# Scores of two mLSTM heads in turn, from the two row halves of the array, and exponents of two heads made ahead

## The chip, the core and the metric

The kernel runs on one core of a Trainium2 chip. Its engines are PE (TensorE: matmuls; PEld is its weight load), DVE (VectorE), ACT (ScalarE), POOL (GpSimd) and SP, which issues loads. The metric is the device time of one launch in microseconds (us). A difference of 0.2% is about what the measurement can tell from none.

## What is computed

A decoder layer on 512 positions of width 1024: an mLSTM branch and a sparse-attention branch, merged by gates, then a gated feed-forward network. The change lies in the mLSTM branch, which has four heads (q and k 64 wide, v 128 wide). The reference works in chunks of 64; what it comes to for one head is

```python
b = jnp.cumsum(logf, axis=-1)
D = b[..., :, None] - b[..., None, :] + i_pre[..., None, :]
D = jnp.where(causal, D, NEG)
m_t = jnp.maximum(inter, jnp.max(D, axis=-1))
Dw = jnp.exp(D - m_t[..., None])
s = jnp.einsum('bhctd,bhcsd->bhcts', q, k) * Dw
num = isc[..., None] * jnp.einsum('bhctd,bhcde->bhcte', q, C_prev) + jnp.einsum('bhcts,bhcse->bhcte', s, v)
h = num / jnp.maximum(jnp.abs(den), jnp.exp(-m_t))[..., None]
```

after which each head is normalised over its 128 columns and multiplied by `sigmoid(mo)`.

## The kernel before, in words

The kernel works on the whole 512x512 lower triangle of a head at once, in tiles of 128x128: four tiles of keys j, and for each the queries i >= j. Products of float32 numbers are made of three matmuls, on a rounded part (h) and a remainder (l): kh·qh, kh·ql, kl·qh.

PE is fed in an order that is written out by hand. Between the steps of a chain the code calls `fill(ns)`, which issues matmuls of an independent stream, in triples of 128x512, until their nominal length (650 for a triple) has used up `ns`. While the heads run, the stream is the projection `gn`: eight tiles gn0 to gn7 of 24 matmuls (lines 489 to 491), two PSUM buffers of the pool `pa` in turn. A finished tile is copied out by ACT (line 709), some triples later in ACT's program order. Its weights are split three tiles ahead by ACT (lines 88 and 91) and a DMA that adds (line 92). Behind the `gn` stream comes the stream `un` (lines 509 to 511). The lengths stand in the table `PLAN`. Each engine executes its own instructions in program order.

One head h goes through these steps (names as in the code and the rows):

- `mls_s`: PE makes the row-max term `mb` with one matmul of 36 rows (line 1087) and the scores with twelve matmuls of 64 rows (lines 1095 to 1097), into two PSUM tiles `mA` and `mB` of the pool `s` (two buffers of two banks). q and k of heads 0 and 2 lie in rows 0 to 63 of a tile `mq`, those of heads 1 and 3 in rows 64 to 127.
- `mls_e` (line 1106): DVE adds `mb` and a column, and takes the minimum with 0, in ten pieces of 128x128, into the SBUF tiles EA and EB. `mls_x`: ACT takes exp of both (lines 1112 and 1113), POOL masks the diagonal tiles (line 1116).
- `mls_m` (lines 1121 and 1122): DVE multiplies scores and exponentials.
- `mls_b`: PE makes the outputs `mo` (line 1129: ten products, each of which runs as two matmuls of 128x129) in the PSUM tiles of the pools `pt` and `po`, which have one buffer each. ACT takes the absolute value of the denominator (1134), DVE a maximum and a reciprocal (1135, 1137), ACT four squares (1142), DVE and ACT the inverse root (`rstd`, lines 382 to 388), and DVE scales into `hs` (1150). In the middle of it, `mid` starts `mls_s`, `mls_e` and `mls_x` of the next head.
- `mls_c`: PE transposes `hs` in four matmuls into `mhT` (line 1158), in the one buffer of `pt`; DVE multiplies it with a gate (1159), ACT and DVE split the product (1160, 1161).

Head 0's scores, exponents and products stand ahead of the loop over heads. Behind head 3's `mls_b` the `gn` stream is run to its end, if it has any left, and `un` takes over.

Of the kernel before, what the change touches and what calls it, by code (L numbers as in the profile page):

```python
# [10 lines left out]
ALU = mybir.AluOpType  # L11
# [4 lines left out]
P = 128  # L16
S = 512
D = 1024
NT = S // P
# [78 lines left out]
def bcast(ap, n):  # L98
# [30 lines left out]
def FL(key, default):  # L129
    return PLAN.get(key, default)  # L130


PD = dict(A=0, C=2, MV=2, GM=2, MO=2, MQK=2, GN=0, UN=0, UM=0, WO=0)

# [26 lines left out]
def body(ctx, tc, I, out, dbg=None):  # L161
    nc = tc.nc
    act, dve, pe, pool = nc.scalar, nc.vector, nc.tensor, nc.gpsimd
# [39 lines left out]
    def lpage(name, dt=F32):  # L203
        return ar.tile([P, 2064], dt, name=name, tag="pm", bufs=1)

    def s4(name, dt=F32):
        return ar.tile([P, 1024], dt, name=name, tag="s4", bufs=6)
# [4 lines left out]
    def psS(name):  # L212
        return ps.tile([P, 1024], F32, name=name, tag="s", bufs=2)
# [13 lines left out]
    T = {}  # L227
# [63 lines left out]
    W.on_pool = {T_B[c] for c in range(4) if FL(f"q2_pb{c}", (1, 0, 0, 0)[c])}  # L291
    for nm, ids in (("A", T_A), ("C", T_C), ("MV", T_MV), ("GM", F_GM), ("MO", F_MO), ("MQK", F_MQK), ("GN", F_GN),
                    ("UN", F_UN), ("UM", F_UM), ("WO", T_WO[:4])):
# [71 lines left out]
    for tl, names in ((vrow, (("merge_gate_b", 16), ("m_conv_w", 16), ("m_conv_b", 4), ("m_out_norm_w", 4))),  # L365
                      (vrow2, (("ffn_conv_w", 3 * NF), ("ffn_conv_b", NF)))):
        r = 0
        for nm, n in names:
            a = I[nm]
# [84 lines left out]
    def tok_accs(name):  # L454
        a0, a1, s = pa(name + "0"), pa(name + "1"), psS(name + "s")
        return [a0[:, :], a1[:, :], s[:, 0:512], s[:, 512:1024]]

    def tok_group(ids, n, accs, evac, flag):
        cost = 650 * n / 512
        W.ensure(ids[0])  # L460
        for c, i in enumerate(ids):
            H, L = W.hl[i]
            order = [(t, kk) for t in range(NT) for kk in range(2)]
            if 0 < c < 3:
                order.sort(key=lambda e: e[1])
            for z, (t, kk) in enumerate(order):
                k = 2 * c + kk
                if z == FL("q8_ens" + flag, 4):
                    W.ensure(i + 3)
                mm3(accs[t][:, :n], act4(hTH, k, t * P, (t + 1) * P), act4(hTL, k, t * P, (t + 1) * P),  # L470
                    H[:, kk, :], L[:, kk, :], k == 0, k == KD - 1)
                if k == KD - 1:
                    d = FL("q4_aft" + flag, 1) + 1
                    after(d, lambda t=t: evac(t, accs[t]))
                    if t == NT - 1:
                        after(d, lambda: done.add(flag))
                yield cost
                tick()
# [255 lines left out]
    def proj_stream():  # L734
        yield from tok_group(T_C, 288, tok_accs("aC"), evac_c, "C")
        yield from tok_group(T_A, 512, tok_accs("aA"), evac_a, "A")
        T["mv1"] = lpage("mv1").rearrange("p (t h c) -> p t h c", t=NT, h=4)
# [10 lines left out]
    fill = Filler(proj_stream(), flush)  # L748
# [329 lines left out]
        dve.tensor_copy(uoc, p[:, 0:40])  # L1078
        act.activation(emc, p[:, 40:56], AF.Exp, scale=-1.0)

    def mls_s(h):
        r0 = slice((h % 2) * 64, (h % 2) * 64 + 64)
        mq = T["mq"][h // 2][r0]
        A = psS(f"mA{h}")
        B = psS(f"mB{h}")
        mb = B[:, 0:512]
        pe.matmul(mb, sel[:, h, :], T["nHL"], start=True, stop=True)
        at = [A[:, 0:512], A[:, 512:896], B[:, 768:1024], B[:, 512:768]]
        for j in range(NT):
            ks = slice(j * P, (j + 1) * P)  # L1090
            kh, kl = mq[:, 1, ks], mq[:, 3, ks]

            q0 = min(j, NT - 2) * P
            qh, ql = mq[:, 0, q0:], mq[:, 2, q0:]
            pe.matmul(at[j], kh, qh, start=True, stop=False)
            pe.matmul(at[j], kh, ql, start=False, stop=False)
            pe.matmul(at[j], kl, qh, start=False, stop=True)
        return A[:, 0:896], B[:, 640:1024], mb

    def mls_e(h, sc):  # L1100
        mb = sc[2]
        EA, EB = s4(f"EA{h}"), s4(f"EB{h}")
        et = [EA[:, 0:512], EA[:, 512:896], EB[:, 128:384], EB[:, 0:128]]
        for k, (i, j) in enumerate(pairs):
            e = et[j][:, (i - j) * P:(i - j + 1) * P]
            dve.tensor_scalar(e, mb[:, i * P:(i + 1) * P], uoc[:, k * 4 + h:k * 4 + h + 1], 0.0,
                              op0=ALU.add, op1=ALU.min)
        return EA[:, 0:896], EB[:, 0:384], et

    def mls_x(ee):  # L1110
        EA, EB, et = ee
        act.activation(EA, EA, AF.Exp)
        act.activation(EB, EB, AF.Exp)
        for j in range(NT):
            e = et[j][:, 0:P]
            pool.affine_select(e, e, pattern=[[1, P]], compare_op=ALU.is_ge, fill=0.0, base=0,
                               channel_multiplier=-1)

    def mls_m(sc, ee):
        EA, EB, et = ee  # L1120
        dve.scalar_tensor_tensor(EA, sc[0], 0.125, EA, op0=ALU.mult, op1=ALU.mult)
        dve.scalar_tensor_tensor(EB, sc[1], 0.125, EB, op0=ALU.mult, op1=ALU.mult)

    def mls_b(h, et, mid):
        o = [pt(f"mo{h}0"), po(f"mo{h}1")]
        ov = [o[i // 2][:, (i % 2) * 129:(i % 2) * 129 + 129] for i in range(NT)]
        for i in range(NT):
            for j in range(i + 1):
                pe.matmul(ov[i], et[j][:, (i - j) * P:(i - j + 1) * P], T["mv1"][:, j, h, :],
                          start=(j == 0), stop=(j == i))  # L1130
        nxt = mid[0]()
        ad = sm([P, 4], "mad")
        for z in range(2):
            act.activation(ad[:, 2 * z:2 * z + 2], o[z][:, :258].rearrange("p (b c) -> p b c", b=2)[:, :, P], AF.Abs)
        dve.tensor_max(ad, ad, emc.rearrange("p (t h) -> p t h", h=4)[:, :, h])
        rec = sm([P, 4], "mrec")
        dve.reciprocal(rec, ad)
        hp = s4(f"hs{h}")
        hs, junk = hp[:, 0:512], hp[:, 512:640]
        ss = sm([P, 4], "mss")  # L1140
        for i in range(NT):
            act.activation(junk, ov[i][:, 0:P], AF.Square, scale=rec[:, i:i + 1],
                           accum_out=ss[:, i:i + 1])
        ne = mid[1](nxt)
        rs = sm([P, 4], "mrs")
        rstd(rs, ss, 4, 1.0 / P)
        mid[2](ne)
        dve.tensor_mul(rs, rs, rec)
        for i in range(NT):
            dve.tensor_scalar(hs[:, i * P:(i + 1) * P], ov[i][:, 0:P], rs[:, i:i + 1], None, op0=ALU.mult)  # L1150
        return hs, nxt, ne
# [36 lines left out]
    fill(FL("z19", 1950))  # L1188
    fill.until(done, "A")

# [50 lines left out]
        fill(FL("z25", 1300))  # L1241
    act.preload_act_table_set(LNEXP)
    T["hmH"] = v4(page("hmH", F32R))
    sc = mls_s(0)
    ee = mls_e(0, sc)
    mls_x(ee)
    fill(FL("ms0", 5000))
    mls_m(sc, ee)
    for h in range(4):
        if h < 3:  # L1250
            mid = (lambda: mls_s(h + 1), lambda n: mls_e(h + 1, n), mls_x)
        else:
            mid = (lambda: None, lambda n: None, lambda n: None)
        fill(FL(f"mb{h}", 1000))
        hs, sc, ee = mls_b(h, ee[2], mid)
        if h == 3:
            fill.until(done, "GN")
            fill = Filler(up_group(F_UN, T["onH"], T["onL"], evac_un, "un", "UN", (1, 3, 6, 7)), flush)
            W.ensure(F_UN[3])
            act.preload_act_table_set("sigmoid_and_others")  # L1260
            for i in range(2):
                for z in range(2):
                    g = T["gn"][i][:, 2 * z:2 * z + 2, :]
                    act.activation(g, g, AF.Sigmoid)
        fill(FL(f"mc{h}", 5000))
        if h == 2:
            mls_m(sc, ee)
        mls_c(h, hs)
        if h == 3:
            for i in range(2):  # L1270
                for z in range(2):
                    fill(1300)
                    g = T["gm"][i][:, 2 * z:2 * z + 2, :]
                    act.activation(g, g, AF.Sigmoid)
            act.preload_act_table_set(LNEXP)
        if h < 2:
            fill(FL(f"md{h}", 2000))
            mls_m(sc, ee)
    fill.until(done, "UN")


# [22 lines left out]
    fill = Filler(up_group(F_UM, T["hmH"], T["hmL"], evac_um, "um", "UM", (1, 6, 7)), flush)  # L1304
# [339 lines left out]
```

## Time and profile before

| | us |
|---|---|
| timed runs | 782.43, 783.40, 783.75 (median 783.4) |
| the profiled execution | 782.3 |
| its span, from the first to the last instruction | 780.6 |
| PE busy | 773.1 (99%) |
| DVE busy | 468.4 (60%) |
| ACT busy | 373.9 (48%) |
| POOL busy | 208.1 (27%) |

The profile is one execution. Busy time is the union of an engine's records. Matmuls are pipelined: a record begins where the matmul is issued and ends, by a model, where its last column has left, so that records overlap and the distance of two starts tells how long one holds the engine. Waits are named by the line that released them. The heads run from 285 to 352 us of the span.

### The profile page before, as it was taken

To read this page: it belongs to the slowest core of one execution; us is meant where nothing else is said; L and a number is where in the kernel's file an instruction comes from. 1 tells how busy PE (TensorE), PEld (TensorE's weight loads), DVE (VectorE), ACT (ScalarE), POOL (GpSimd) and SP (SyncE) were. 2 spreads that over 40 slices of the span, in tenths; PEclk is the share of its full clock that TensorE was granted. 3 is DMA by queue.
4 is the path that set the end of the run, shared out by engine and by line. 5 is a ranking of instruction groups with operands and counts; after the bars stand their busy time and mean duration, and the time that the engine had idled before them with its cause. 6 is when DMAs were issued, how large, how long until landed. Compare 5 with 4: busy or idle time off the path is not lost.

```text
span 780.6 us, 10546 instructions
## 1 busy us (share of the span) xinstructions
PE 773.1 (99%) x4037; PEld 641.0 (82%) x4037; DVE 468.4 (60%) x826; ACT 373.9 (48%) x630; POOL 208.1 (27%) x220
## 2 busy tenths in 40 slices
PE   8999999999999999999999999999999999999998
PEld 6797888778888888888888988888888888888886
DVE  5476785676566664566627365555545454566865
ACT  6254546645565685475624253333443433455441
POOL 3320131220111122110200037745555542200700
PEclk9999999999999999999999999999999999999999
DMA  6984069665656476543687168664455533675472
GB/s 232 295 224 140 7 127 170 109 110 107 109 100 117 87 104 135 107 136 108 145 290 249 45 217 307 226 246 171 182 216 193 183 122 150 213 276 185 148 237 87
DMA packets 93892, 129.03 MB, mean 165 GB/s; under 512 B 6512, under 2 KB 72208, under 8 KB 92433
## 3 DMA queue, kind: packets, MB, share of 16 engines
q1 hardware_dynamic: 63054, 91.64, 35.0%
q0 software_dynamic: 30784, 36.70, 22.8%
q8 instruction: 32, 0.52, 0.3%
q14 instruction: 20, 0.16, 0.1%
q10 hardware_dynamic: 2, 0.00, 0.0%
HBM read 94.79 MB, written 15.73 MB: 142 GB/s over the span
## 4 chain that ended last, share of the span: by engine, by line
PE 93%; DVE 4%; issue 1%; ACT 1%; POOL 0%; DVEq 0%; POOLq 0%
PE ff L1361 10%; PE ff L1360 10%; PE ff L1359 10%; PE P L428 4%; PE P L429 4%; PE P L427 4%; PE on L937 2%; PE ptp L926 2%; PE gn L489 2%; PE gn L491 2%; PE gn L490 2%; PE wo L429 2%; PE wo L428 2%; PE wo L427 2%; PE gm L489 1%; PE gm L491 1%
## 5 line engine op out<-in xcount | busy, mean ns | idle before, releaser
L94 DVE TENSOR_TENSOR whl<-raw,whl 128x1024 fp32r<-128x1024 f32 (+2 forms) x109 | 137.7, 1275 | 149.8 <-ACT whl L88 149.7
L88 ACT ACTIVATE whl<-raw 128x1024 fp32r<-128x1024 f32 (+2 forms) x144 | 144.8, 1012 | 126.4 <-PE ff L1361 57.3
L1359 PE MATMUL ff<-h2H,whl 128*128 128x512 f32 (+1 forms) x384 | 142.8, 372 | 0.0
L1360 PE MATMUL ff<-h2L,whl 128*128 128x512 f32 (+1 forms) x384 | 142.6, 371 | 0.0
L1361 PE MATMUL ff<-h2H,whl 128*128 128x512 f32 (+1 forms) x384 | 142.6, 371 | 0.0
L92 POOL DMA_DIRECT2D whl<-raw x34 | 47.0, 1384 | 231.8 <-ACT whl L91 181.5
L1360 PEld LDWEIGHTS ff<-h2L,whl 128*128 128x128 f32 x384 | 72.3, 188 | 12.6
L1359 PEld LDWEIGHTS ff<-h2H,whl 128*128 128x128 f32 x384 | 72.3, 188 | 12.5
L1361 PEld LDWEIGHTS ff<-h2H,whl 128*128 128x128 f32 x384 | 72.3, 188 | 12.4
L911 ACT ACTIVATE P<-sp,nmx 128x128 f32<-128x128 f32 (+3 forms) x64 | 33.1, 523 | 36.8 <-DVE nmx L902 36.5
L1411 ACT ACTIVATE ct<-ct 128x512 f32<-128x512 f32 x22 | 13.9, 633 | 54.1 <-DVE ct L1409 54.1
L902 DVE TENSOR_REDUCE nmx<-sp 128x2 f32<-128x256 f32 (+3 forms) x32 | 26.2, 818 | 17.9 <-PE sp L899 17.8
L91 ACT ACTIVATE whl<-raw 128x1024 fp32r<-128x1024 f32 x34 | 35.7, 1050 | 0.0
L427 PE MATMUL P<-whl,g 128*128 128x512 f32 x88 | 34.2, 389 | 0.0
L428 PE MATMUL P<-whl,g 128*128 128x512 f32 x88 | 34.2, 389 | 0.0
L429 PE MATMUL P<-whl,g 128*128 128x512 f32 x88 | 34.2, 389 | 0.0
L1409 DVE SCALAR_TENSOR_TENSOR ct<-ff,vcol,ct 128x511 f32<-128x511 f32 (+1 forms) x44 | 32.7, 744 | 2.2 <-ACT ct L1407 1.4
L1417 ACT ACTIVATE g<-ct 128x512 fp32r<-128x512 f32 x22 | 13.9, 632 | 36.9 <-DVE ct L1421 21.9
L235 DVE COPY P<-ptp 128x256 f32<-128x256 f32 (+1 forms) x32 | 17.7, 554 | 18.6 <-PE ptp L926 18.5
L1418 DVE TENSOR_TENSOR g<-ct,g 128x512 fp32r<-128x512 f32 x22 | 15.4, 699 | 21.9 <-ACT g L1417 21.9
L489 PE MATMUL gm<-hTH,whl 128*128 128x512 f32 x64 | 26.6, 416 | 0.0
L428 PE MATMUL P<-whl,sb 128*128 128x512 f32 x66 | 25.9, 393 | 0.2
(399 smaller groups left out, 1781.0 us busy)
## 6 DMA issues: line engine op xcount, KB each, us to landing
raw<-in_ffn_w_up_dram SPq DMA_DIRECT2D x22, 1024.0 KB, 5.0
whl<-raw POOLq DMA_DIRECT2D x34, 512.0 KB, 5.7
raw<-in_w_in_dram SPq DMA_DIRECT2D x16, 1024.0 KB, 5.0
st<-in_ffn_w_down_dram SPq DMA_DIRECT2D x11, 1024.0 KB, 7.1
td<-st POOLq DMA_DIRECT2D x11, 1024.0 KB, 4.1
raw<-td SPq DMA_DIRECT2D x22, 512.0 KB, 5.3
raw<-in_ffn_w_down_dram SPq DMA_DIRECT2D x11, 512.0 KB, 4.1
raw<-in_w_out_dram SPq DMA_DIRECT2D x4, 1024.0 KB, 4.7
```

The lines of the kernel that those rows point to most:

```text
L88: nc.scalar.activation(h, src, AF.Copy)
L91: nc.scalar.activation(l, src, AF.Copy, scale=-1.0)
L92: nc.gpsimd.dma_start(l, src, accum_op=ALU.add)
L94: (nc.gpsimd if n in self.on_pool else nc.vector).tensor_sub(l, src, h)
L427: pe.matmul(o, aH, bH, start=start, stop=False)
L428: pe.matmul(o, aH, bL, start=False, stop=False)
L429: pe.matmul(o, aL, bH, start=False, stop=stop)
L489: pe.matmul(acc, H[:, k, :], hh, start=(k == 0), stop=False)
L911: act.activation(Pv[:, y], sv[:, y], AF.Exp, bias=nmx[:, y:y + 1], accum_out=den[:, y:y + 1])
L1359: pe.matmul(acc[:, a:b], H[:, k, :], hh, start=(k == 0), stop=False)
L1360: pe.matmul(acc[:, a:b], H[:, k, :], hl, start=False, stop=False)
L1361: pe.matmul(acc[:, a:b], L[:, k, :], hh, start=False, stop=(k == KD - 1))
```

## The change

The scores of heads 0 and 1, and of heads 2 and 3, are issued in turn, one matmul of the lower and one of the upper row half. `mls_sA` makes the tiles j = 0 and 1 of two heads (each head in a PSUM tile of its own) and multiplies them; `mls_sB` does the same for j = 2 and 3 (one PSUM tile, a bank for each head). The row-max matmul gets a PSUM tile of its own (`mls_mb`), and DVE's exponent pieces read it there. Ahead of the loop, row-max terms and exponents of heads 0 and 1 are made, then their scores. Inside `mls_b` of heads 0 and 1 the row-max term and the exponents of heads 2 and 3 follow; their scores stand behind `mls_c(1)`. Fillers are spread anew.

```diff
-    "mc0": 4675, "mc1": 5000, "mc2": 5000, "mc3": 11500, "md0": 3950, "md1": 3625, "md2": 0, "ms0": 6300,
+    "mc0": 5850, "mc1": 5850, "mc2": 5850, "mc3": 11500, "md0": 3900, "md1": 1950, "md2": 34800, "ms0": 6500,
...
-    def mls_s(h):
...
+    def mls_mb(h):
+
+        mb = psS(f"mM{h}")[:, 0:512]
         pe.matmul(mb, sel[:, h, :], T["nHL"], start=True, stop=True)
...
+    def mls_s(p, js, at):
+
+        mq = T["mq"][p]
+        for j in js:
+            ks = slice(j * P, (j + 1) * P)
+
+            q0 = min(j, NT - 2) * P
+            for n, (kk, qq) in enumerate(((1, 0), (1, 2), (3, 0))):
+                for z in range(2):
+                    r = slice(z * 64, z * 64 + 64)
+                    pe.matmul(at[z][j], mq[r, kk, ks], mq[r, qq, q0:], start=(n == 0), stop=(n == 2))
+
+    def mls_sA(p, ees):
+        A = [psS(f"mA{2 * p + z}") for z in range(2)]
+        mls_s(p, (0, 1), [(a[:, 0:512], a[:, 512:896]) for a in A])
+        for z in range(2):
+            dve.scalar_tensor_tensor(ees[z][0], A[z][:, 0:896], 0.125, ees[z][0], op0=ALU.mult, op1=ALU.mult)
+
+    def mls_sB(p, ees):
+        B = psS(f"mB{p}")
+        b = [B[:, z * 512:z * 512 + 512] for z in range(2)]
+        mls_s(p, (2, 3), [{2: a[:, 256:512], 3: a[:, 0:256]} for a in b])
+        for z in range(2):
+            dve.scalar_tensor_tensor(ees[z][1], b[z][:, 128:512], 0.125, ees[z][1], op0=ALU.mult, op1=ALU.mult)
...
-    sc = mls_s(0)
-    ee = mls_e(0, sc)
-    mls_x(ee)
-    fill(FL("ms0", 5000))
-    mls_m(sc, ee)
+    none = (lambda: None, lambda n: None, lambda n: None)
+    mbs = [mls_mb(z) for z in range(2)]
+    ees = {z: mls_e(z, mbs[z]) for z in range(2)}
+    for z in range(2):
+        mls_x(ees[z])
+    fill(FL("ms0", 6500))
+    mls_sA(0, (ees[0], ees[1]))
+    fill(FL("ms1", 1950))
+    mls_sB(0, (ees[0], ees[1]))
+    fill(FL("ms2", 1300))
     for h in range(4):
-        if h < 3:
-            mid = (lambda: mls_s(h + 1), lambda n: mls_e(h + 1, n), mls_x)
-        else:
-            mid = (lambda: None, lambda n: None, lambda n: None)
-        fill(FL(f"mb{h}", 1000))
-        hs, sc, ee = mls_b(h, ee[2], mid)
+        mid = none
+        if h < 2:
+            mid = (lambda: mls_mb(h + 2), lambda n: mls_e(h + 2, n), mls_x)
+        hs, _, ne = mls_b(h, ees[h][2], mid)
+        if h < 2:
+            ees[h + 2] = ne
...
-        if h == 2:
-            mls_m(sc, ee)
         mls_c(h, hs)
...
-        if h < 2:
+        if h == 1:
+            mls_sA(1, (ees[2], ees[3]))
+            fill(FL("ms3", 2600))
+            mls_sB(1, (ees[2], ees[3]))
+        if h < 3:
             fill(FL(f"md{h}", 2000))
-            mls_m(sc, ee)
```

On PE at the start of the heads, before: behind the row-max matmul and the scores of head 0 come 30 fillers (the rest of gn1, gn2, three of gn3), then head 0's outputs.

```order
L1087 MATMUL mB0_2879<-mrowC_1771,sel_176 128x512 [waits Pool_49]
L1095 MATMUL mA0_2878<-mq0_2813 128x512 [waits Activation_49]
L1096 MATMUL mA0_2878<-mq0_2813 128x512 [waits DVE_49]
...
L1097 MATMUL mB0_2879<-mq0_2813 128x256
L489 MATMUL gn1_2835<-hTH1_140,whl33_2634 128x512
...
L489 MATMUL gn3_2944<-hTH0_139,whl35_2817 128x512 [waits Activation_49]
...
L1129 MATMUL mo00_2950<-mv1_944,EA0_2893 128x129 [waits DVE_49,PE_49]
```

The same place now: two row-max matmuls, 30 fillers, and the scores of heads 0 and 1 in turn.

```order
L1084 MATMUL mM0_2878<-mrowC_1771,sel_176 128x512 [waits Pool_49]
L1084 MATMUL mM1_2880<-mrowC_1771,sel_176 128x512
L489 MATMUL gn1_2835<-hTH1_140,whl33_2634 128x512
...
L489 MATMUL gn3_2951<-hTH0_139,whl35_2817 128x512 [waits Activation_49]
L490 MATMUL gn3_2951<-hTL0_141,whl35_2817 128x512
L491 MATMUL gn3_2951<-hTH0_139,whl35_2817 128x512 [waits DMASW7_49]
L1106 MATMUL mA0_2955<-mq0_2813 128x512 [waits DVE_49,PE_49]
L1106 MATMUL mA1_2956<-mq0_2813 128x512 [waits DVE_49,PE_49]
```

The scores moved from ahead of the fillers to behind them; gn3, which waits for ACT, stands 27 fillers behind the row-max matmuls, as it stood 27 behind the scores.

On ACT at the same place, before: the exponentials of head 0, then the copy of filler tile gn1.

```order
L1242 ACT_TABLE_LOAD
L1112 ACTIVATE EA0_2893<-EA0_2893 128x896 [waits DVE_49]
L1113 ACTIVATE EB0_2894<-EB0_2894 128x384 [waits DVE_49,Activation_49]
L709 ACTIVATE gn0_2794<-gn1_2835,vcol_132 128x512 [waits PE_49]
L88 ACTIVATE whl37_2928<-raw18_2734 128x1024 [waits DMASW5_49]
```

And now:

```order
L1248 ACT_TABLE_LOAD
L1123 ACTIVATE EA0_2882<-EA0_2882 128x896 [waits DVE_49]
L1124 ACTIVATE EB0_2883<-EB0_2883 128x384 [waits DVE_49,Activation_49]
L1123 ACTIVATE EA1_2894<-EA1_2894 128x896 [waits DVE_49,Activation_49]
L1124 ACTIVATE EB1_2895<-EB1_2895 128x384 [waits DVE_49]
L709 ACTIVATE gn0_2794<-gn1_2835,vcol_132 128x512 [waits PE_49]
L88 ACTIVATE whl37_2935<-raw18_2734 128x1024 [waits DMASW5_49]
```

The copy of gn1 moved behind the exponentials of two heads.

On PE at the end of the heads, before: between head 2's outputs (`mo2`) and its transposes (`mhT2`) stand head 3's row-max matmul and scores and 24 fillers; between the transposes and head 3's outputs (`mo3`) stand 12.

```order
L1129 MATMUL mo21_3222<-mv1_944,EB2_3126 128x129 [waits Pool_49]
L1087 MATMUL mB3_3234<-mrowC_1771,sel_176 128x512
L1095 MATMUL mA3_3233<-mq1_2814 128x512
...
L489 MATMUL gn6_3205<-hTH1_140,whl38_3035 128x512
...
L491 MATMUL gn7_3310<-hTH0_139,whl39_3074 128x512
L1158 MATMUL mhT2_3326<-ident_96,hs2_3254 128x128 [waits DVE_49,Activation_49]
...
L489 MATMUL gn7_3310<-hTH1_140,whl39_3074 128x512
...
L1129 MATMUL mo30_3352<-mv1_944,EA3_3260 128x129 [waits DVE_49,Pool_49]
```

The same place now: 9 fillers, the last of gn7, in the first gap, none in the second, and behind head 3's outputs the stream un.

```order
L1135 MATMUL mo21_3297<-mv1_944,EB2_3035 128x129 [waits Pool_49]
L489 MATMUL gn7_3259<-hTH1_140,whl39_3088 128x512
...
L491 MATMUL gn7_3259<-hTH1_140,whl39_3088 128x512
L1164 MATMUL mhT2_3346<-ident_96,hs2_3314 128x128 [waits DVE_49,Activation_49]
L1164 MATMUL mhT2_3346<-ident_96,hs2_3314 128x128
L1164 MATMUL mhT2_3346<-ident_96,hs2_3314 128x128 [waits DVE_49] x2
L1135 MATMUL mo30_3354<-mv1_944,EA3_3162 128x129 [waits DVE_49,Pool_49]
...
L1135 MATMUL mo31_3355<-mv1_944,EB3_3163 128x129 [waits Pool_49]
L509 MATMUL un0_3402<-onH_1543,whl40_3129 128x512
```

The scores of head 3 and 27 fillers moved out of this stretch to places ahead of it.

## Rows read from the trace of the kernel before

**Rows 1.** The page, the chain that ended last, by engine.

```profile
PE 93%; DVE 4%; issue 1%; ACT 1%; POOL 0%; DVEq 0%; POOLq 0%
```

**Rows 2.** Windows: stretch, length, busy us of PE, PEld, DVE, ACT, POOL, PEclk, DMA.

```profile
285.00:339.40 54.40, 54.34 (x295) 45.78 (x293) 30.53 (x93) 33.34 (x71) 13.01 (x22) 1.00 0.63 118
```

**Rows 3.** Timeline of PE, head 0: start, length, line, tiles, shape.

```profile
284.50 0.39 PE L491 MATMUL gn<-hTH,whl 128*128 128x512 f32 x1
...
285.18 0.39 PE L491 MATMUL gn<-hTH,whl 128*128 128x512 f32 x1
285.50 0.50 PE L1087 MATMUL mB<-mrowC,sel 36*128 36x512 f32 x1
285.83 0.40 PE L1095 MATMUL mA<-mq 64*128 64x512 f32 x1
...
287.07 0.28 PE L1095 MATMUL mB<-mq 64*128 64x256 f32 x1
...
288.20 0.39 PE L490 MATMUL gn<-hTL,whl 128*128 128x512 f32 x1
```

**Rows 4.** Timeline of PE, head 1.

```profile
296.60 0.61 PE L1129 MATMUL mo<-mv,EB 128*128 128x129 f32 x4
297.14 0.49 PE L1087 MATMUL mB<-mrowC,sel 36*128 36x512 f32 x1
297.14 0.49 PE L1095 MATMUL mA<-mq 64*128 64x512 f32 x1
297.48 0.39 PE L1096 MATMUL mA<-mq 64*128 64x512 f32 x1
...
299.62 0.39 PE L490 MATMUL gn<-hTL,whl 128*128 128x512 f32 x1
```

**Rows 5.** Timeline of DVE, head 0.

```profile
285.45 1.29 DVE L1236 TENSOR_TENSOR mq<-cv,mq 128x512 fp32r<-128x512 f32 x2 [1.08 <-ACT mq L1233]
287.98 1.90 DVE L1106 TENSOR_SCALAR EA<-mB,uoc 128x128 f32<-128x128 f32 x7 [1.23 <-PE mB L1097]
289.79 0.86 DVE L1106 TENSOR_SCALAR EB<-mB,uoc 128x128 f32<-128x128 f32 x3
```

**Rows 6.** Timeline of ACT, head 0.

```profile
290.77 0.51 ACT L1113 ACTIVATE EB<-EB 128x384 f32<-128x384 f32 x1
291.19 0.67 ACT L709 ACTIVATE gn<-gn,vcol 128x512 f32<-128x512 f32 x1
```

**Rows 7.** Timeline of all engines, head 3's outputs and `hs`.

```profile
339.01 0.61 PE L1129 MATMUL mo<-mv,EB 128*128 128x129 f32 x4
...
339.69 0.40 PE L510 MATMUL un<-onL,whl 128*128 128x512 f32 x1
...
344.05 1.13 DVE L1150 TENSOR_SCALAR hs<-mo,mrs 128x128 f32<-128x128 f32 x4
```

**Rows 8.** Timeline of all engines, head 0's `hs` and transposes.

```profile
303.64 1.13 DVE L1150 TENSOR_SCALAR hs<-mo,mrs 128x128 f32<-128x128 f32 x4
...
303.95 0.39 PE L491 MATMUL gn<-hTH,whl 128*128 128x512 f32 x1
...
304.40 0.76 PE L1158 MATMUL mhT<-ident,hs 128*128 128x128 f32 x4
...
304.91 0.48 PE L489 MATMUL gn<-hTH,whl 128*128 128x512 f32 x1
...
305.19 0.75 DVE L1159 SCALAR_TENSOR_TENSOR hs<-mhT,vcol,mo 128x512 f32<-128x512 f32 x1 [0.42 <-PE mhT L1158]
```

**Rows 9.** Timeline of PE, the start, to the longest idle of PE.

```profile
10.69 0.63 PE L428 MATMUL aB<-whl,hTH 128*128 128x512 f32 x1
11.11 0.44 PE L429 MATMUL aB<-whl,hTL 128*128 128x512 f32 x1
11.39 0.39 PE L427 MATMUL aB<-whl,hTH 128*128 128x512 f32 x1
...
14.01 0.31 PE L420 MATMUL pn<-ident,x 128*128 128x128 f32 x1 [0.38 <-issue]
```

More of the change, by code (lines that the diff above doesn't have):

```diff
@@ L1079, in rows_b, with mls_e @@
         act.activation(emc, p[:, 40:56], AF.Exp, scale=-1.0)
-    def mls_s(h):
[L1082 to L1086, printed above, removed]
-        pe.matmul(mb, sel[:, h, :], T["nHL"], start=True, stop=True)
[L1088 to L1101, printed above, removed]
+    def mls_mb(h):
+        mb = psS(f"mM{h}")[:, 0:512]
+        pe.matmul(mb, sel[:, h, :], T["nHL"], start=True, stop=True)
+        return mb
+    def mls_e(h, mb):
         EA, EB = s4(f"EA{h}"), s4(f"EB{h}")
@@ L1117, in mls_x @@
                                channel_multiplier=-1)
[L1119 to L1122, printed above, removed]
     def mls_b(h, et, mid):
```

## Prediction

> **What bounds the kernel now.** I read the page first: its chain that ended last is 93% PE [rows 1]. A busy PE need not be a well-used one, so next I asked for the stretch of the four mLSTM heads by windows: PE busy 54.34 of 54.40 us, PEclk 1.00, DVE and ACT busy for 30.53 and 33.34 us [rows 2]. So PE sets the end here. What an edit saves on PE comes off the end, what makes PE wait goes onto it, and work on DVE or ACT counts only where PE waits for it. Matmul records overlap (their ends are modelled), so from here on I read PE by its starts: a 128x512 filler matmul starts every 0.227 us, (285.18-284.50)/3 [rows 3].
>
> The PE timeline of head 0 prices one block of scores [rows 3]. From the last filler at 285.18 to the second filler behind the block at 288.20 are 3.02 us; less two filler steps that is 2.57. Inside: 0.227 for the row-max matmul (36 rows); 1.24 for the six matmuls of 512 and 384 columns (285.83 to 287.07), called A; and, since 285.18 to 285.83 is two normal steps and 0.20, 0.20 for entering; the remaining 0.90 is the six of 256 columns, B, and leaving. I take leaving at 0.20 too, so B is 0.70, and one change to the half-height rows and back costs 0.40. Head 2 repeats this. Head 1, whose q and k lie in rows 64 to 127, is cheaper: four output matmuls from 296.60 at 0.112 end their turn at 297.05, so to 299.62, less one filler step, it takes 2.34 [rows 4]; head 3 repeats that. All four: 2x2.57+2x2.34 = 9.82 us.
>
> **What the pairing saves.** Why head 1 is cheaper is the best row there is for the pairing. Its row-max matmul (rows 0 to 35) and its first score matmul (rows 64 up) both start at 297.14, both last 0.49, and the next one follows at 297.48 [rows 4]. One alone took as long, 285.50 to 285.83 [rows 3]. So two 512-column matmuls in different row halves, weight loads included, ran in the time of one. I take that for all 24 pairs. After the change there are seven blocks: one with two row-max matmuls (both in rows 0 to 35, so in turn: 0.45+0.40 = 0.85), two with one (0.63 each), two A (1.24+0.40 = 1.64 each) and two B (0.70+0.40 = 1.10 each). Sum 0.85+1.26+3.28+2.20 = 7.59, against 9.82: 2.23 us saved. Bounds: if pairs do not overlap, A and B cost twice their 1.24 and 0.70, the sum is 11.47 and the change loses 1.65 here. The other end is the 2.23 plus the three additional changes of rows, 1.2, should they come free. I keep 2.23, since [rows 4] show the very case.
>
> The trace has only single such meetings, not a run of them. The Trainium skill (TensorE: Matmul & The Clock Gate, "Measured speedup vs the span model") gives 3.07x for four row tiles, not 4x. At that share of the ideal, two tiles would give an estimated 1.54x, each pair of heads would cost 2x1.94/1.54 = 2.52 instead of 1.94, and 1.1 us would be saved instead of 2.23; that is 787.3, inside the forecast's own range below. The row shows no loss, so the sum goes by the row.
>
> A wait of PE goes too: the transposes of head 0 started 0.45 after the last filler instead of 0.227 [rows 8], 0.22 us. Behind the change head 0's chain has 27 fillers and a row-max block to hide it, about 6.6 us of PE from the end of its output matmuls. That chain is 5.2 us (below), or about 5.7 with the exponents of a later head in DVE's way; the wait does not come back there, nor for head 1, which has the same cover. I count -0.22.
>
> **What the longer start costs.** The exponents of two heads now stand at the start. DVE ends its last step on q and k at 285.45+1.29 = 286.74; ten exponent pieces take 2.67 (287.98 to 289.79+0.86), twenty 5.3, so the second head's are there at 292.0 instead of 290.65 [rows 5]. Then ACT's second Exp on EB1 starts, 0.51; and in ACT's queue the copy of filler tile gn1 (L709, 0.67) now stands behind it. It started 0.42 after the Exp began [rows 6]; now that is 292.5, and it ends at 293.1 instead of 291.86. Filler tile gn3 takes gn1's PSUM buffer. PE comes to it after the two row-max matmuls and 27 fillers: second filler at 285.83+0.227+0.20+0.227 = 286.48, then 26x0.227, so 292.4. With the wake-up and a weight load PE waits some 0.8 us (0.4 to 1.1). Before, PE came to gn3 at 288.20+26x0.227 = 294.1, two us behind that copy. The rest of the start hides: nothing else in ACT's queue is late for PE, and score block B waits for DVE's multiply on A's buffer behind nine fillers (2.0 us against 1.1 and its latency).
>
> **What runs out at the end.** The order shows that the fillers are spent sooner: before, 24 of them and a score block stood between head 2's output matmuls and its transposes, and 12 more before head 3's outputs. Now 9 stand in the first place and none in the second. The chain from outputs to transposes has its length in head 3 of before, which has no next head inside: last output record ends at 339.01+0.61 = 339.62, hs begins at 344.05, 4.43 us [rows 7]; the transposes start 0.76 after hs does (303.64 to 304.40) [rows 8]. Together 5.19. PE's next stream counts from 0.16 before that record's end (its second matmul at 339.69, less 0.227) [rows 7], so nine fillers cover 9x0.227-0.16 = 1.88. PE stands still for 3.3 us (2.9 to 3.6). Nothing can jump in: the transposes wait at the head of PE's queue.
>
> Directly behind them stand head 3's outputs, which need the one `pt` buffer that the transposes have just filled. Transposes from 304.40 to the next start at 304.91 with its usual first gap of 0.1 count to about 304.95; DVE's product reads the buffer from 305.19 for 0.75, to 305.94 [rows 8]; a wake-up and a load add 0.15. PE waits 1.15 us (0.9 to 1.4). Before, 12 fillers, 2.7 us, hid it. Everything behind (the un stream, the last transposes) hangs on head 3's outputs as before and shifts with them. DMAs: the loads on SP's queue wait for the same conversions, none of which comes late by this; I count nothing.
>
> **Sum:** -2.23-0.22+0.8+3.3+1.15 = +2.8 us on the profiled execution, 782.3 to 785.1. That execution lies 1.1 under the median of the timed runs, 783.4, so the forecast is 786.2.
>
> **Rivals.**
> The pairs do not overlap in a run: +1.65 instead of -2.23, so +6.7, 790.1. For it: no steady run of pairs in the trace; against it: 297.14. 7%.
>
> The clock falls. PE's longest idle anywhere is 0.38 us, at 14.01 [rows 9], and the granted clock of the heads is 1.00, the 2.4 GHz level [rows 2]. Now PE would be still for 3.3 us, do four transposes and be still for 1.15. At the start a 128x512 step took 0.42 (10.69 to 11.11) [rows 9], the 1.2 GHz level, and that low stretch was at most 11 us long, so a fall costs at most 5.5 and more likely 2 to 4: 788.2 to 790.2. The Trainium skill (TensorE: Matmul & The Clock Gate, "HAM oscillation — how this bites in real kernels") says that idle gaps between bursts bring the clock back down; no run here shows one that does. 10%.
>
> Changing rows is cheap: the 0.40 may belong to a block's semaphore waits, of which the new blocks have fewer. Then up to seven blocks lose most of it against four, and the gain grows by some 1.5: +1.3, 784.7, no difference to speak of. Against it: head 2's block, with other waits, has the same price. 13%.
>
> The end goes the other way, faster: head 2's transposes do not wait, so both end terms go together and -2.23-0.22+0.8 = -1.65 is left, 781.7. It needs the chain from outputs to transposes under 1.9 us, or another filler in its place; it decides from there. Against it: the four squares on ACT alone are two of its 5.19 us and the change leaves them there. For it: only that I might misplace the fillers in time. 9%.
>
> The forecast as summed, 785.0 to 787.4, has the remaining 61%.
>
> **How the numbers follow.** 0.2%, about what a measurement tells from no change, is 1.57 us, so same is 781.8 to 785.0. Faster is the last rival and little else: 0.09. Same is the cheap change of rows and a small end of the forecast: 0.17. Slower is the rest of the forecast, the missing overlap and the clock: 0.74. The range 783.4 to 789.0 leaves out the faster rival, the missing overlap and the upper part of the clock's.
>
> **What would show it.** Right: on PE, the two scores of a pair start together and A takes about 1.2 us for two heads; a wait of 3 us before head 2's transposes with hs (DVE) as its releaser, one of about 1.2 before head 3's outputs, and one of under 1 at gn3 released by ACT's L709; the un stream's second matmul stands about 2.8 us behind 339.69. Wrong: A of 2.5 us (no overlap); steps of 0.42 in head 3's outputs or un (clock); or a wait at another place, above all before the transposes of heads 0 and 1.

## The result, and the profile after

| us | before | after |
|---|---|---|
| timed runs | 782.38 to 783.75, median 783.29 (5) | 786.77 to 789.86, median 789.27 (5) |
| the profiled execution | 782.3 | 789.27 |
| its first row-max matmul starts | 285.50 | 287.39 |
| the second matmul of un starts | 339.69 | 346.65 |
| between these two | 54.20 | 59.26 |
| from there to the last instruction | 440.91 | 440.92 |

The change makes the kernel slower: ratio 1.0073 (1.0062 to 1.0084), +6.0 us, against a forecast of +2.8. Differences are taken before the starts are rounded. The last rows of the table say where to look: behind the heads nothing differs, and the heads (from the first row-max matmul to the second matmul of un) are 5.06 us longer. 1.89 us more stood there before the heads began, in a stretch where both kernels issue the same instructions.

First the terms that the prediction summed. The timeline of PE, the first pair; columns are start, length, engine, line, tiles, shape, count and, in brackets, the idle time with its releaser:

```profile
294.09 0.39 PE L491 MATMUL gn<-hTH,whl 128*128 128x512 f32 x1
295.13 0.50 PE L489 MATMUL gn<-hTH,whl 128*128 128x512 f32 x1 [0.65 <-ACT gn L709]
...
295.70 0.40 PE L491 MATMUL gn<-hTH,whl 128*128 128x512 f32 x1
296.02 1.49 PE L1106 MATMUL mA<-mq 64*128 64x512 f32 x12
...
297.78 0.39 PE L490 MATMUL gn<-hTL,whl 128*128 128x512 f32 x1
...
299.40 0.39 PE L491 MATMUL gn<-hTH,whl 128*128 128x512 f32 x1
299.71 0.98 PE L1106 MATMUL mB<-mq 64*128 64x256 f32 x12
...
300.96 0.40 PE L490 MATMUL gn<-hTL,whl 128*128 128x512 f32 x1
```

Read as in [rows 3], two filler steps taken off: A is 297.78-295.70-0.45 = 1.63 us (1.64 forecast), B 300.96-299.40-0.45 = 1.11 (1.10), each for two heads. The wait at gn3 is 295.13-294.09-0.23 = 0.81 (0.8 forecast), released by L709 as it said. The timeline of PE at the end of the heads:

```profile
336.73 0.39 PE L491 MATMUL gn<-hTH,whl 128*128 128x512 f32 x1
340.18 1.08 PE L1164 MATMUL mhT<-ident,hs 128*128 128x128 f32 x4 [3.06 <-DVE hs L1156]
342.20 2.49 PE L1135 MATMUL mo<-mv,EA 128*128 128x129 f32 x10 [0.94 <-DVE hs L1165]
...
346.34 0.48 PE L509 MATMUL un<-onH,whl 128*128 128x512 f32 x1
346.65 0.39 PE L510 MATMUL un<-onL,whl 128*128 128x512 f32 x1
```

Both forecast waits stand where they should: 3.22 us before head 2's transposes (340.18-336.73-0.23; 3.3 forecast) and a shorter one before head 3's outputs. But head 3's twenty output matmuls take 4.14 us from 342.20 to un, where in the kernel before they took 339.38-337.23 = 2.15:

```profile
337.23 1.28 PE L1129 MATMUL mo<-mv,EA 128*128 128x129 f32 x10
...
339.38 0.48 PE L509 MATMUL un<-onH,whl 128*128 128x512 f32 x1
```

The windows of after (stretch, length, busy us of PE, PEld, DVE, ACT, POOL, PEclk, DMA) name the reason:

```profile
285.00:335.00 50.00, 49.35 (x270) 39.43 (x270) 27.73 (x81) 31.87 (x59) 13.04 (x22) 1.00 0.80 154
336.90:340.10 3.20, 0.22 (x1) 0.00 (x0) 1.66 (x9) 1.71 (x7) 0.00 (x0) 0.88 0.00 0
339.35:346.18 6.83, 5.07 (x22) 4.72 (x23) 2.57 (x6) 0.80 (x2) 0.00 (x0) 0.50 0.02 4
```

PE is still from about 337.0 on, and from 339.35, 0.8 us before the transposes, the granted clock is 0.50, the 1.2 GHz level, for 6.83 us; in [rows 2] it is 1.00 throughout. So the rival "the clock falls" came on top of the forecast.

### The profile page after: what moved, and what is told of

It is laid out like the page before. It is cut to its first block, busy times and chain, and to the rows that moved or that the text cites. A ratio compares the mean times of both kernels' runs of the same rounds, so it can differ in the third digit from the quotient of the medians.

```text
span 787.6 us, 10544 instructions
## 1 busy us (share of the span) xinstructions
PE 773.9 (98%) x4037; PEld 639.5 (81%) x4037; DVE 468.8 (60%) x826; ACT 374.3 (48%) x630; POOL 207.3 (26%) x220
## 4 chain that ended last, share of the span: by engine, by line
PE 88%; DVE 5%; ACT 2%; SPq 1%; issue 1%; DMA 1%; DVEq 0%; ACTq 0%
PE ff L1371 10%; PE ff L1373 10%; PE ff L1372 10%; PE P L428 4%; PE P L429 4%; PE P L427 4%; PE on L937 2%; PE ptp L926 2%; PE wo L427 2%; PE wo L428 2%; PE wo L429 2%; PE gm L489 1%; PE gm L491 1%; PE gm L490 1%; PE sp L896 1%; PE mo L1135 1%
## 5 line engine op out<-in xcount | busy, mean ns | idle before, releaser
L489 PE MATMUL gn<-hTH,whl 128*128 128x512 f32 x64 | 26.0, 406 | 0.7 <-ACT gn L709 0.7
```

The source lines that it names most:

```text
L489: pe.matmul(acc, H[:, k, :], hh, start=(k == 0), stop=False)
```

## Experiments

The result is from one job, the experiments from three later ones. Times of one job are compared with the runs of the kernel before in that job (median 782.94, 783.06 and 782.70 us). "Heads" is the stretch of the table's fifth row.

**The changed kernel again.** No edit.

> The changed kernel, unaltered, a second profile and five more times. Its profiled run was 6.97 us longer than that of the kernel before. Read so far: 1.86 us of it already at 21 us, where PE waited for the third block of x; some 3.0 us the sum of the prediction; 2.1 us a stretch of 6.8 us at granted clock 0.50 behind the wait before head 2's transposes. Theory A (the clock falls in that wait every time; the late x is an accident of the one run): a low stretch stands at the same place in this profile too, 3.4 or 6.8 us long, PE's eighth pn transpose group starts near 21.3 us or near 23.1 us whatever the clock does, and the times are 786.5 to 790. Theory B (the low clock is an accident of the one run): this profile shows 1.00 throughout the heads, and most times lie near 786. Theory C (the changed kernel makes x late): x is late by 1.8 us again.

788.25 us (786.54 to 788.96), ratio 1.0063 (1.005 to 1.0075). Heads 59.33 us; its timeline of PE and its window:

```profile
339.20 0.75 PE L1164 MATMUL mhT<-ident,hs 128*128 128x128 f32 x4 [3.06 <-DVE hs L1156]
340.88 2.49 PE L1135 MATMUL mo<-mv,EA 128*128 128x129 f32 x10 [0.94 <-DVE hs L1165]
```

```profile
340.15:346.98 6.83, 6.10 (x24) 5.79 (x25) 1.62 (x4) 1.75 (x7) 0.00 (x0) 0.50 0.01 2
```

Theory A: a low stretch of 6.83 us is there again. It reaches into un, where it costs another 0.6 (441.52 us from un's second matmul to the end, against 440.92). But it begins at 340.15, 0.95 us behind the start of the transposes, so in the second wait and not in the first as above. The start is 286.42 this time.

**The gap filled with useless matmuls.**

```diff
         fill(FL(f"mc{h}", 5000))
+        if h == 2:
+            dummy(24)
         mls_c(h, hs)
+        if h == 2:
+            dummy(8)
```

> The changed kernel with 24 additional matmuls of 128x128x256 (of the identity, into a PSUM tile that nobody reads; some 0.114 us each, 2.7 us) in PE's wait before head 2's transposes, and 8 (0.9 us) in the wait before head 3's outputs. The data waits stay as long as they were, PE is only not still in them. Theory A (the clock's fall is a cost of its own, on top of the waits): granted clock 1.00 throughout the heads, head 3's outputs take 2.2 us instead of 4.1, and the time is 786.5 to 787.3, 2 to 2.8 under the changed kernel's 789.3. Rival B (the low clock covers time that PE would have waited anyway): the same 789.3 within 0.5. Rival C (the clock falls by itself in this stretch whatever PE does): a low stretch in this profile as well.

785.86 us, 2.4 under the changed kernel in the same job; ratio 1.0034 (1.0022 to 1.0047). The timeline of PE:

```profile
335.57 3.03 PE L1253 MATMUL dummy<-identr 128*128 128x256 f32 x24
338.80 0.76 PE L1164 MATMUL mhT<-ident,hs 128*128 128x128 f32 x4 [0.19 <-DVE hs L1156]
339.31 1.19 PE L1253 MATMUL dummy<-identr 128*128 128x256 f32 x8
340.49 1.35 PE L1135 MATMUL mo<-mv,EA 128*128 128x129 f32 x10
...
342.71 0.48 PE L509 MATMUL un<-onH,whl 128*128 128x512 f32 x1
```

and its window:

```profile
285.00:342.00 57.00, 56.15 (x321) 45.68 (x320) 30.40 (x93) 34.31 (x72) 13.04 (x22) 1.00 0.68 135
```

The data waits are as long as they were, the clock stays at 1.00, the outputs take 342.71-340.49 = 2.22. Theory A (its range in us, 786.5 to 787.3, was counted from the first job's 789.3; from this job's 788.25 the drop is the 2 to 2.8 that it gave). Heads 57.03 us, 2.83 more than before: with the clock held, what is left is the prediction's own sum. As both waits are filled here, this doesn't say which of the two the fall needs.

**The same gap in the kernel before.**

```diff
-    "mc0": 4675, "mc1": 5000, "mc2": 5000, ...
+    "mc0": 4675, "mc1": 5000, "mc2": 650, ...
```

> The kernel before, without any pairing, with 21 of its fillers moved from ahead of head 2's transposes to behind them (3 instead of 24 there, 33 instead of 12 before head 3's outputs). PE has 2.9 us of work then behind head 2's outputs, against a chain of 5.7 to its transposes, so it waits some 2.9 us. Theory A (a PE that waits so long brings the granted clock down, whatever else the kernel does): a low stretch behind the wait, in which the fillers go at 0.43 us a step instead of 0.227; 2.9 us for the wait and 2 to 3.4 for the clock, 787.8 to 789.3. Rival B (the fall needs the changed kernel's further waits, at gn3 or before head 3's outputs): no low stretch, 785.9.

788.87 us, ratio 1.0074 (1.0061 to 1.0086). Timelines of PE and DVE, and the window of its low stretch:

```profile
328.86 0.40 PE L491 MATMUL gn<-hTH,whl 128*128 128x512 f32 x1
333.40 1.09 PE L1158 MATMUL mhT<-ident,hs 128*128 128x128 f32 x4 [4.15 <-DVE hs L1150]
...
334.72 0.63 PE L490 MATMUL gn<-hTL,whl 128*128 128x512 f32 x1
335.14 0.63 PE L491 MATMUL gn<-hTH,whl 128*128 128x512 f32 x1
```

```profile
328.40 1.90 DVE L1106 TENSOR_SCALAR EA<-mB,uoc 128x128 f32<-128x128 f32 x7 [1.55 <-PE mB L1097]
...
330.99 0.16 DVE L382 TENSOR_SCALAR rs_v<-mss 128x4 f32<-128x4 f32 x1
```

```profile
330.68:337.50 6.82, 4.10 (x12) 3.46 (x13) 5.22 (x16) 4.19 (x7) 2.33 (x5) 0.50 0.08 13
```

Theory A in kind: without pairs, and with no second wait behind it, one wait of this length alone brings the clock down, and a filler step is 335.14-334.72 = 0.42 us. The sizes were off: I gave the wait 2.9 us, it is 333.40-328.86-0.23 = 4.3, because in the kernel before the next head's exponents wait for its scores too (they share the tile mB, and its last score matmul, L1097, releases them), and stand in DVE's queue ahead of the inverse root (L382) and hs. Of the 6.24 us that the heads grew, 4.3 is the wait, and 1.9 is left for the clock; that the time lies in theory A's range is in part luck, as a longer wait made up for a cheaper fall. A single wait of 3.2 us wasn't tried.

**The gap half filled.** `dummy(12)` behind the nine fillers, none before head 3's outputs.

> The changed kernel with 12 additional matmuls (128x128x256, 0.114 us each, 1.4 us, into a tile that nobody reads) directly behind the nine fillers ahead of head 2's transposes, none before head 3's outputs. The data waits are as in the changed kernel, but PE is still for 1.7 us instead of 3.1 in the first, and for 0.9 in the second. In other runs a PE wait of 1.7 us (behind head 0's outputs, first spreading) and one of 1.9 (at the start of the changed kernel's profiled run) left the granted clock at 1.00. Theory A (it is the length of one wait that decides, and 1.7 us isn't enough): clock 1.00 throughout the heads, the time of the kernel with the gap wholly filled, 785.9 (785.4 to 786.4). Rival B (two waits near each other count together): a low stretch behind head 2's transposes, 787.5 to 788.5.

Undecided between the two: 785.10 and 785.73 us with mean clock 0.999, and 787.74 to 789.22 with 0.996 or 0.997 in the other four. The profiled one is a run without the fall, heads 57.01 us:

```profile
338.19 0.75 PE L1164 MATMUL mhT<-ident,hs 128*128 128x128 f32 x4 [1.64 <-DVE hs L1156]
339.88 1.35 PE L1135 MATMUL mo<-mv,EA 128*128 128x129 f32 x10 [0.93 <-DVE hs L1165]
```

A program in whose one trace PE is still for 1.64 and then 0.93 us loses the clock in some runs and not in others. Where it fell in those four no trace shows; their mean clock and time are all there is. In the changed kernel all eleven executions had a mean clock of 0.995 to 0.997.

**Fillers spread again.** Same instructions, other places.

```diff
-    "mc0": 5850, "mc1": 5850, "mc2": 5850, ... "md0": 3900, ... "ms0": 6500,
+    "mc0": 5850, "mc1": 5850, "mc2": 5200, ... "md0": 1300, ... "ms0": 5200, "ms2": 650,
```

> The changed kernel with the same instructions, but its fillers spread again: 24 instead of 30 before A of the first pair, 3 instead of 6 before head 0's outputs, 6 instead of 18 before head 1's outputs, 24 instead of 9 before head 2's transposes, 6 instead of 0 before head 3's outputs. Theory A (the loss is the three waits of PE and the clock that falls in the longest): the waits of 0.8, 3.2 and 0.9 us at gn3, before head 2's transposes and before head 3's outputs are gone, the clock stays at 1.00, the pairing's 2.2 us and the 0.2 of head 0's transposes are what is left, and the time is 780.9 (780 to 782), 2.4 faster than the kernel before. Rival B (the pairs themselves lose, and the waits only show it): no faster than the kernel before, 783 or more.

782.59 us, ratio 0.9994 (0.9985 to 1.0003): neither 780.9 nor quite the rival, no difference from the kernel before. Clock 1.00, heads 54.00 us. The timeline of PE shows a wait that I had made myself:

```profile
304.12 0.39 PE L491 MATMUL gn<-hTH,whl 128*128 128x512 f32 x1
306.05 0.50 PE L489 MATMUL gn<-hTH,whl 128*128 128x512 f32 x1 [1.55 <-ACT gn L709]
```

306.05-304.12-0.23 = 1.70 us. The timeline of ACT shows what the copy stood behind:

```profile
304.08 0.94 ACT L1123 ACTIVATE EA<-EA 128x896 f32<-128x896 f32 x1
304.92 0.51 ACT L1124 ACTIVATE EB<-EB 128x384 f32<-128x384 f32 x1
305.33 0.67 ACT L709 ACTIVATE gn<-gn,vcol 128x512 f32<-128x512 f32 x1
```

It is the mechanism of the forecast's gn3 term, at another head: head 0's outputs had come 9 fillers earlier in the order, so ACT's copy now stood behind head 0's squares and head 2's Exps.

**Fillers spread a second time.**

```diff
-    "mc0": 5850, "mc1": 5850, "mc2": 5850, ... "md0": 3900, ... "ms0": 6500,
+    "mc0": 5200, "mc1": 5850, "mc2": 5200, ... "md0": 1300, ... "ms0": 5850, "ms2": 650,
```

> The fillers spread once more. In the first spreading the pairing's gain was eaten by a wait that it made itself: behind head 0's outputs PE stood 1.7 us at a gn tile, for ACT's L709 copy of the tile two before it, which stood in ACT's queue behind head 0's squares and head 2's Exps. Here 27 fillers stand before A of the first pair (24 there), 24 behind head 0's outputs (27 there), so that this copy is issued before head 0's outputs. Theory A (nothing but waits hid the gain): no wait over 0.3 us among the heads; from the first row-max matmul to the second matmul of un some 52.1 us (54.2 in the kernel before, 54.0 in the first spreading, 57.0 with the gap filled), and the time is 780.8 (780.3 to 781.5), 2.1 under the kernel before. Rival B (the pairs themselves save nothing): 782.5 or more, as in the first spreading.

780.94 us (7 runs), ratio 0.9971 (0.996 to 0.9982): faster than the kernel before, where the changed one is slower. The clock is 1.00. Heads 51.94 us. Timeline of PE, the first pair's A and the end of the heads:

```profile
293.63 0.39 PE L491 MATMUL gn<-hTH,whl 128*128 128x512 f32 x1
293.95 1.50 PE L1106 MATMUL mA<-mq 64*128 64x512 f32 x12
295.38 0.50 PE L489 MATMUL gn<-hTH,whl 128*128 128x512 f32 x1
...
334.21 0.60 PE L1164 MATMUL mhT<-ident,hs 128*128 128x128 f32 x4
...
335.81 0.40 PE L491 MATMUL gn<-hTH,whl 128*128 128x512 f32 x1
336.34 1.35 PE L1135 MATMUL mo<-mv,EA 128*128 128x129 f32 x10
```

A is followed at once by gn3, whose copy has had A's time to finish. Of the 2.45 us that pairing and head 0's lost wait were to save, 2.26 arrive; some 0.3 (336.34-335.81-0.23) is a wait before head 3's outputs that six fillers don't quite cover.

**What the pairs are worth.** Three orders of the same score matmuls. First, within each A and B, three of one head before three of the other, on the first spreading:

```diff
-            for n, (kk, qq) in enumerate(...):
-                for z in range(2):
+            for z in range(2):
+                for n, (kk, qq) in enumerate(...):
```

> As the kernel with the fillers spread again, but within A and B the three matmuls of one head are issued before the three of the other, so that neighbours in the queue lie in the same rows of the array except where the head changes. Theory A (two score matmuls in different row halves run at the same time, in the time of one): each A goes from 1.24 to some 2.4 us and each B from 0.70 to 1.3, less what the four changes of head in a block still overlap; the time is 2.5 to 3.9 us over that of the kernel with the fillers spread again. Rival B (the gain was in fewer changes to half-height rows, not in pairs): within 0.5 us of it.

782.64 us against 782.59, heads 54.02 against 54.00: theory A's time failed, because the edit didn't take the overlap away. The timeline of PE at the second A, cut at 320.30, shows two score matmuls starting together. Two of the same rows start 0.23 us apart or more at this size, so the second is the other head's first, the fourth in the queue:

```profile
320.15 0.50 PE L1106 MATMUL mA<-mq 64*128 64x512 f32 x2
```

Blocks last as long as in the first spreading: the first A 1.71 us in both traces, the second 1.50 against 1.49. So this run, whose time is what rival B said, doesn't decide between the two.

Then all six of one head before the six of the other, on the second spreading (`for z` outermost):

> As the second spreading, but in A and B all six matmuls of one head are issued before the six of the other. With three and three the records showed the first of one head and the first of the other, fourth in the queue, starting within 0.01 us of each other, and no loss. Theory A (TensorE's queue runs ahead without a limit that matters here, so two row halves overlap whatever the order in a block): the same time as the second spreading within 0.4 us, and the first matmuls of both heads start together. Rival B (it looks only a few matmuls ahead, or starts them in order): the seventh starts after the third or later, an A takes 0.6 to 1.2 us more, a B 0.35 to 0.7, the time is 1.9 to 3.9 us more.

782.11 us against 780.94, heads 53.75 against 51.94. Timeline of PE; the first row is that of a narrow stretch that ends at 293.20:

```profile
292.52 1.07 PE L1105 MATMUL mA<-mq 64*128 64x512 f32 x4
...
292.52 2.07 PE L1105 MATMUL mA<-mq 64*128 64x512 f32 x12
294.52 0.50 PE L489 MATMUL gn<-hTH,whl 128*128 128x512 f32 x1
```

Rival B in kind: A takes 2.00 us instead of 1.43, and by 293.20 four had started, where one head alone would have started three and pairs six. So the fourth to start is the other head's first, the seventh in the queue, ahead of the fourth to sixth. The time is only 1.2 us more (heads 1.8), less than the 1.9 that it gave at least. Last, three fillers between the two heads' sixes:

> As the second spreading, but in A and B the second head's six matmuls stand three fillers behind the first head's six, so that no two of different row halves can meet; the number of fillers is the same. Theory A (the pairing saves by overlap, and each change to half-height rows and back costs 0.40 us): 2x(1.24+0.70) = 3.9 us for the lost overlap and 4x0.40 = 1.6 for four more changes, 5.5 us more than the second spreading. Rival B (the halves do not save time, records only overlap on paper): 1.6 us more, from the changes alone.

786.06 us; heads 57.40, 5.46 more than the second spreading (5.5 expected, theory A), with the clock at 1.00 and no wait of PE that the timeline shows. Timeline of PE, the second pair's A, head by head:

```profile
320.60 1.49 PE L1107 MATMUL mA<-mq 64*128 64x512 f32 x6
322.02 0.50 PE L489 MATMUL gn<-hTH,whl 128*128 128x512 f32 x1
...
322.91 1.50 PE L1107 MATMUL mA<-mq 64*128 64x512 f32 x6
324.34 0.50 PE L489 MATMUL gn<-hTH,whl 128*128 128x512 f32 x1
```

Six matmuls of one head hold PE for 322.02-320.60 = 1.42 us; the twelve of two heads above for 1.43.

**The start.** The kernel before twice more, and the changed one a third time, one execution each.

> The kernel before, unaltered, for a second trace of its first 286 us. There the two kernels issue the same instructions, yet the first row-max matmul stands at 285.50 in the trace of before, at 285.35 in the variant of it with a gap, and at 285.5 to 287.4 in seven traces of the changed kernel and its variants. Theory A (an accident of each run, when the third block of x lands): here anywhere between 285.3 and 287.4. Rival B (the changed kernel makes its own start later): 285.3 to 285.6 again.

> As the run before it, a third trace of the kernel before, with the same two expectations: anywhere between 285.3 and 287.4 us (accident), or 285.3 to 285.6 again (made by the change).

> The changed kernel, unaltered, a third trace. Accident: its first row-max matmul anywhere between 285.3 and 287.4; made by the change: 286.4 or later again, as in its first two traces (287.40, 286.42). In both cases, from that matmul to the second matmul of un 59.3 us within 0.2, and a low stretch of the clock behind the wait before head 2's transposes, as in the first two.

First row-max matmul at 285.48 (782.30 us) and 286.79 (783.74 us) in the kernel before: a late start comes without the change too. The wait is for the load of the third block of x, which ACT's square of that block (L399) waits for: 0.79, 0.75 and 1.97 us in the three traces of the kernel before, 2.52, 1.68 and 1.58 in those of the changed one. Whether the changed kernel has late starts more often isn't shown; in five traces of its variants PE doesn't wait there. Heads 54.20 and 54.21. The timelines of PE in the slower of these two, and in the changed kernel's first trace:

```profile
22.58 1.06 PE L420 MATMUL pn<-ident,x 128*128 128x128 f32 x8 [1.29 <-DVE x L412]
```

```profile
23.13 1.06 PE L420 MATMUL pn<-ident,x 128*128 128x128 f32 x8 [1.88 <-DVE x L412]
```

In the changed kernel's third trace the start is 286.19 and the heads take 58.46, not 59.3: the low stretch was shorter there,

```profile
340.27:343.68 3.41, 3.03 (x14) 3.06 (x15) 0.93 (x2) 0.80 (x2) 0.00 (x0) 0.50 0.02 5
```

## Why the prediction was too low

**What held.** The side, and every term of the sum. Blocks: A 1.63, B 1.11 as forecast. The waits: 0.81 at gn3, 3.22 before head 2's transposes; before head 3's outputs, with the clock held by the dummies, 340.49-338.80 = 1.69 from the transposes on, of which four filler-free steps of about 0.1 are work, so some 1.3 (1.15 forecast; it is 1.69 without dummies too, 339.88-338.19 with the gap half filled). Head 0's transposes no longer wait. Together +2.83 in the kernel with the gap filled, against +2.8; its median is 2.9 over that of before. The Trainium skill (TensorE: Matmul & The Clock Gate, "Measured speedup vs the span model") gives 3.07x for four row tiles. Here two row tiles ran at the full 2x (twelve matmuls in 1.43 us, six in 1.42), so the estimate of 1.54x made from it doesn't hold for this case.

**The step that failed.** It is "PE stands still for 3.3 us", with 1.15 us more behind it, followed by a sum in which everything after goes at full clock: the clock's term was put at nothing. I named the fall as a rival, priced it about right (2 to 4 us on top, 788.2 to 790.2) and then gave it 10%, and cut the range at 789.0. It was the likeliest case: the fall came in all eleven executions of the changed kernel, and in the kernel before when it was given such a wait. In the traces it cost 59.26-57.03 = 2.2 us, 2.9 (59.33-57.03, and 0.6 in un) and 1.4; between medians of one job 2.4. Which of the two waits it needs stays open: it came in the first wait in one trace and behind the transposes in two; one wait of 4.3 us was enough in the kernel before with a gap, and 1.64 and 0.93 us were in four executions of six. My evidence against it was that the clock was 1.00 everywhere and PE's longest idle 0.38 us [rows 2, 9], which says only that the trace held no wait of that kind. The Trainium skill (TensorE: Matmul & The Clock Gate, "HAM oscillation — how this bites in real kernels") says that idle gaps between bursts bring the clock down. I set it aside because no row showed one, and the trace after agrees with it, 0.50 for 6.83 us.

**Smaller.** 2.8 and 2.3 make 5.1 us; the second job shows 5.3, the first 6.0. The profiled execution of the first had the late x block, 1.9 us of its 6.97. That the timed runs of that job had more of such starts was not tried; they left no traces. What their mean clocks do show: of the eleven executions, the five with 0.997 (the trace with a low stretch of 3.41 us is one) took 786.54 to 787.90 us, the six with 0.995 or 0.996 (the two traces with 6.83 us are among them) 788.25 to 789.86. So two of the first five executions, 786.77 and 786.82, lay in the forecast's range although the clock fell in them too.

## What to carry to other kernels

A wait of PE of some microseconds, opened in a stream that had none, had two prices here: its own length, and a slower clock behind it. A trace without such a wait says nothing on the second price, so the forecast of a change that opens one should have it in its sum, or at least in its range. A change of order is judged only with its fillers laid out for it: the same pairs cost 6 us, nothing, or gained 2, by where 147 filler matmuls stood and which copy stood behind which Exp in ACT's queue.

## What was not expected of the hardware

- TensorE started matmuls ahead of earlier ones in its queue where they lie in the other half of the rows: the fourth together with the first, without loss (heads 54.02 and 54.00 us). So "Each engine executes its own instructions in program order", said of the kernel before, isn't right for such matmuls. It has an end: with six of one half ahead the seventh started beside the third, and A took 2.00 us instead of 1.43.
- A program with PE still for 1.64 and 0.93 us in its one trace kept the clock up in two runs and had it down in four; with 3.06 and 0.94 us (three traces) it was down in all eleven, for 3.41 or 6.83 us in the traces, and the fall came before the transposes in one trace, behind them in two.
- PE waited 1.29 us for the third block of x in one of three traces of the kernel before, and 1.88, 0.74 and 0.69 us in the three of the changed kernel; in the kernel before that made 783.74 us against 782.30.
